# The first range's padding at the end of its scan, and the gate's last 32 channels standing twice in its weights

## The chip, the cores and the metric

The kernel runs on one core of one Trainium2 chip. The metric is the device time of one execution in microseconds; the time of a kernel is the median of its runs. The core's engines are TensorE (PE, with its weight loads shown apart as PEld), VectorE (DVE), ScalarE (ACT), GpSimd (POOL) and SyncE (SP), which issues most DMAs.

## The reference

Two layers of a decoder trunk on 512 tokens, with 16 learned meta tokens ahead of them (T = 528), width 1024. Each layer is half a SwiGLU, a mixer, half a SwiGLU, each on a normalised input and added to the residual. The mixer of layer 0, which the change touches, is RWKV-7 time mixing; the mixer of layer 1 is sparse attention.

```
def rwkv7_time_mix(h, mix, w_r, w_k, w_v, w_o, w0, w1, w2, a0, a1, a2, g1, g2, k_k, k_a, r_k, lnx_g, lnx_b):
    xx = jnp.pad(h, ((0, 0), (1, 0), (0, 0)))[:, :-1] - h          # token before, less this one
    xm = h[None] + xx[None] * mix[:, None, None, :]                # six mixed inputs
    xr, xw, xk, xv, xa, xg = ...
    r, k, v = xr @ w_r, xk @ w_k, xv @ w_v
    w_log = -softplus(-(w0 + tanh(xw @ w1) @ w2)) - 0.5
    a = sigmoid(a0 + (xa @ a1) @ a2)
    g = sigmoid(xg @ g1) @ g2                                      # g1: 1024 x 160, g2: 160 x 1024
    ...                                                            # kk normalised by head, k, decay
    y = wkv7_scan(r, decay, k, v, -kk, kk * a)                     # 16 heads, a 64 x 64 state each
    ...                                                            # group norm of y, bonus r*k*r_k*v
    return ((yn + bonus) * g) @ w_o

def step(S, inp):                                                  # of wkv7_scan, one token
    sa = einsum("bhij,bhj->bhi", S, a_t)
    S = S * w_t + sa * b_t + v_t * k_t
    y = einsum("bhij,bhj->bhi", S, r_t)
```

## The kernel before

**Products.** Every large product is done in three: both operands are split into a rounded high half and a low half (`split`: ACT rounds, DVE subtracts), and `mm3` issues high x high, high x low and low x high into the same accumulator. Weights come as units of 128 x 1024 from one packed array, in the order in which they are used (`Weights`); SP loads `wraw`, ACT rounds it to `whi`, DVE subtracts to `wlo`. `W.take` hands out the blocks and issues the rounding and splitting two units ahead, so the places of the weight splits in ACT's and DVE's program order follow from the takes. PE accumulators are banks named `acc` (4 of them, main work), `bg` (3, side work and gates) and `ry`.

**Ranges and stages.** The tokens are worked in two ranges, A (tokens 0 to 271) and B (272 to 527). The order is: feed-forward 0,0 of A; projections of A (`proj`, stage pA); feed-forward 0,0 of B (stage f00b); output projection of A (`outproj`, oA); projections of B (pB); feed-forward 0,1 of A (f01a); output projection of B (oB); then layer 1.

**Padding.** The scan works in chunks of `CH` = 32 tokens. A has 272 tokens, eight and a half chunks; it gets 16 empty columns (`pad`) ahead of its first token, so that n = 288 and the chunk numbered 0 is half empty. B has n = 256, eight chunks.

**Side chains.** Beside a main stage run generators (`beside`): `prep` (decay powers, keys), `lmat` (for each chunk the masked products of keys and receptances, into `R.G`), `inverse`, `scan`, `bonus` and `post` (group norm). The order of all instructions is fixed while the program is built: `run` asks a planner with prices for each engine (`Clock`) when a chain's next step would be ready, and puts it between two products of the main stage. `drain` issues what is left of the chains at the end of f00b and of f01a, ahead of oA and oB. Every engine then works through its own instructions in that order.

**Inverse.** For each chunk and head a unit triangular 32 x 32 matrix must be inverted. `lmat` writes the matrices to memory with one partition for each pair of chunk and head; `inverse` loads them (16 partitions a chunk), runs through t = `t0` .. 30 with two DVE instructions each, stores the result and loads it back into `R.G`. It does so by parts, `R.parts`, tuples of first chunk, last chunk, and in the kernel before the first row `t0`: for A chunk 0 alone with t0 = 16 (15 steps on 16 partitions), then chunks 1 to 8 (31 steps on 128 partitions); for B chunks 0 to 7 in one part. The scan of a chunk waits for its part; at c = 0 and at each fourth chunk it also waits for the last part before it takes its output tile `ynat`, since the inverse uses tiles of that name. `post` uses a tile `prod`, as the inverse does.

**Scan.** For each chunk: products of the state `S` and of the masked matrices into `ry`, a copy `rs`, a product with the inverse, the new values `uv`, the output into `ynat`, the new state, which is multiplied by the chunk's whole decay `R.PC`. After chunks 3, 7 and the last one, `bonus` and `post` of up to four chunks are put beside.

**Gate.** 160 channels are padded to 256. At the end of `proj` the first matrix is taken as tiles of 128 and of 32 weight columns (lines 938 to 949), and the sigmoid of both goes to `R.sg`. In `outproj` (lines 1270 to 1313) `R.sg` is split to `lhi`, `llo`, and for each of the 8 column tiles `gate(m)` issues three products with 128 rows and three with 32 rows, then a DVE multiply (`tb`), an ACT rounding (`o_hi`) and a DVE subtraction (`o_lo`). Three gates go first; then, for each d, a gate three ahead and the nine products of output tiles 0 to 2 with operand d; after that output tiles 3 to 7.

Of the kernel before, what the change touches and what calls it, by code (L numbers as in the profile page):

```python
# [10 lines left out]
F32 = mybir.dt.float32  # L11
# [6 lines left out]
D = 1024  # L18
DT = 8
# [414 lines left out]
def trunk(ctx, tc, wall, units, h0, vec, cstd, gqk, out, stop=None, gap=0.0, share=400.0, slack=200.0, fulls={}):  # L434
# [67 lines left out]
    def split(hi, lo, src, gp=False):  # L502
        nc.scalar.activation(hi, src, AF.Copy)
        if gp:
            nc.gpsimd.tensor_tensor(lo, src, hi.bitcast(F32), op=OP.subtract)
        else:
            nc.vector.tensor_sub(lo, src, hi.bitcast(F32))
# [278 lines left out]
    class Range:  # L786
        def __init__(self, r):
            self.r = r
            self.pad = 16 if r == A else 0
            self.n = r[1] - r[0] + self.pad  # L790
            self.nch = self.n // CH
            self.have = set()

            self.parts = [(0, 1, 16), (1, 9, 0)] if self.pad else [(0, 8, 0)]
            self.L, self.T = {}, {}

# [5 lines left out]
    def proj(R, norm, sp, core, XB):  # L802

        r, n, pad, nch = R.r, R.n, R.pad, R.nch
        hn2 = [core.tile([128, 4, 1 + 288], F32, name="ynat", bufs=2) for _ in range(2)]
# [10 lines left out]
        xx = [core.tile([128, 4, 288], F32, name="bu", bufs=2) for _ in range(2)]  # L816
        xm, late = {}, []

        def mix(i, d):

            x = work.tile([128, 288], F32, name="tb", bufs=4)
            nc.vector.scalar_tensor_tensor(x[:, :n], xx[d // 4][:, d % 4, :n], col(MIX + 8 * i + d),
                                           hn[d][:, 1:1 + n], op0=OP.mult, op1=OP.add)
            hi = sp.tile([128, 288], F32R, name="xm_hi", bufs=XB)
            lo = sp.tile([128, 288], F32R, name="xm_lo", bufs=XB)

            def make():
                split(hi[:, :n], lo[:, :n], x[:, :n], gp=True)
# [9 lines left out]
        def mixes(k):  # L838
            while k and queue and free[0]:
                i, d = queue.pop(0)  # L840
                if i == 2:
                    norm.apply(d, r, hn[d][:, 1 + pad:1 + n])
                    nc.vector.tensor_sub(xx[d // 4][:, d % 4, :n], hn[d][:, 0:n], hn[d][:, 1:1 + n])
                mix(i, d)
                if i == 2 and pad:
                    nc.vector.tensor_copy(hnlast[:, d], hn[d][:, n:n + 1])
                free[0] -= 1
                k -= 1
# [56 lines left out]
        for kind, *st in proj_steps():  # L905
# [16 lines left out]
            elif kind == "lora":  # L922
                key, d = st
                if pl is None:
                    pl = bbank("ry")
                mm3(pl[:, :n], W.take(blk(key, d, 0)), need(mixof[key], d), st == ["lw", 0], st == ["la", DT - 1])
                free[0] += 1
                mixes(1)
                if st == ["la", DT - 1]:
                    lora_end(pl)  # L930
                yield
            elif kind == "wa2":
                decay(st[0])
# [20 lines left out]
    def prep(R, core):  # L954
# [7 lines left out]
        def pieces(m, p):  # L962
# [18 lines left out]
            nc.scalar.activation(R.PC[:, :nch, m, 0], R.P[:, m, :nch, 32], AF.Copy, scale=math.exp(UP))  # L981
# [74 lines left out]
    def inverse(R, core):  # L1056

        def load(i):
            L = core.tile([128, CH, CH], F32, name="ynat", bufs=2)
            nc.gpsimd.dma_start(L[:16 * (R.parts[i][1] - R.parts[i][0])], R.L[i].rearrange("p c q s t -> (p c q) s t"))  # L1060
            return L
# [6 lines left out]
        for i, (c0, c1, t0) in enumerate(R.parts):  # L1068
# [4 lines left out]
            TT = core.tile([128, CH, CH], F32, name="ynat", bufs=2)  # L1073
            pr = core.tile([128, 1024], F32, name="prod")
            nc.gpsimd.memset(TT[:k], 0.0)
            nc.gpsimd.memset(TT[:k].rearrange("p s t -> p (s t)")[:, 0:1024:33], 1.0)
            yield 5000
            work = 0
            for t in range(t0, CH - 1):
                a, b = t + 1 - t0, CH - 1 - t  # L1080
                pv = pr[:k, :a * b].rearrange("p (a b) -> p a b", b=b)
                dst = TT[:k, t0:t + 1, t + 1:CH]
                nc.vector.tensor_tensor(pv, TT[:k, t0:t + 1, t:t + 1].to_broadcast([k, a, b]),
                                        L[:k, t:t + 1, t + 1:CH].to_broadcast([k, a, b]), op=OP.mult)
                nc.vector.tensor_add(dst, dst, pv)
                work += 150 + 2.1 * a * b
                if work > 500:
                    yield -500
                    work = 0
            nxt = load(i + 1) if ("L", i + 1) in R.have else None  # L1090
            nc.gpsimd.dma_start(R.T[i].rearrange("p c q s t -> (p c q) s t"), TT[:k])
            for n0, n1 in ((c0, c0 + 1), (c0 + 1, c1)):
                for par in range(2):
                    if n0 < n1:
                        nc.gpsimd.dma_start(R.G[64 * par:64 * par + 32, n0:n1, :, 0:32]
                                          .rearrange("s c q t -> s (c q) t"),
                                          R.T[i][par, n0 - c0:n1 - c0].rearrange("c q s t -> s (c q) t"))
            beside(there(i))

    def scan(R, core, S):  # L1100
# [21 lines left out]
        for c in range(R.nch):  # L1122
# [22 lines left out]
            if c % 4 == 3 or not more:  # L1145
                beside(bonus(R, c - c % 4, c % 4 + 1))
# [123 lines left out]
    def outproj(R, sp, nxt):  # L1270

        n, pad, r = R.n, R.pad, R.r
        shi = sp.tile([128, 2, 288], F32R, name="lhi")
        slo = sp.tile([128, 2, 288], F32R, name="llo")
        for i, k in ((0, 128), (1, 32)):
            split(shi[:k, i, :n], slo[:k, i, :n], R.sg[:k, i, :n])
        xs = {}

        def gate(m):
            p = bbank()  # L1280
            for k, q in ((0, 128), (1, 32)):
                w = W.take(blk("g2", k, m))
                mm3(p[:, :n], (w[0][:q], w[1][:q]), (shi[:q, k, :n], slo[:q, k, :n]), k == 0, k == 1)
# [8 lines left out]
        def end(m, p):  # L1292
            residual(m, r, p[:, pad:n], 1.0)
            nxt.add(m, r)
# [437 lines left out]
def lay_out(i):  # L1732
# [24 lines left out]
    mats["g1"] = pad(f["rk_g1"][0], D, 256)  # L1757
    mats["g2"] = pad(f["rk_g2"][0], 256, D)
# [27 lines left out]
```

## Time and profile before

| | us |
|---|---|
| median of 3 runs | 2370.86 (2370.77 to 2374.3) |
| the profiled execution | 2373.61, its span 2371.8 |
| PE busy in it | 2298.7 |
| DVE busy | 1702.1 |
| ACT busy | 1238.7 |
| POOL busy | 169.6 |
| mean granted clock of PE | 0.979 |

How to read it: a row of a timeline has the start, the length, the engine, the line, the operation, and the output and inputs by their names with shapes; in square brackets stands how long the engine was idle before it and what ended that. Products are written weights x rows, then the moving operand: 32*128 32x288 has 32 rows, 128 weight columns and 288 moving columns. Lengths of products overlap, so the pace is read from starts. PEclk is the granted clock as a share of the full one. All instructions carry line 341, that of the recording helper, so they are told apart by their names. In the profile `bg<-lhi,whi` and its like are the gates' products, `acc<-o_hi,whi` the output projection's, `bg<-pa,bd` and `bg<-pb,bd` the bonus's, `bg<-ident,ynat` the transposes of the normalised output.

### The profile page before, as it was taken

How to read it: one execution, taken by the hardware profiler on the slowest of the kernel's cores; microseconds unless marked ns; L12 is line 12 of the kernel's file. 1: busy time of each engine (PE TensorE's matmuls, PEld its weight loads, DVE VectorE, ACT ScalarE, POOL GpSimd, SP SyncE). 2: the span in 40 equal slices, each digit the busy share in tenths (PEclk: the TensorE clock that was granted, in tenths of full speed). 3: DMA queues.
4: the chain of work that ended last, by engine and by line, in shares of the span. 5: the costliest groups of instructions: out<-in, count | busy, mean ns of one | idle time of the engine just before them, and what ended most of it. 6: DMA issues, size and time to landing. Idle time of an engine off the chain costs nothing.

```text
span 2371.8 us, 49461 instructions
## 1 busy us (share of the span) xinstructions
PE 2298.7 (97%) x20122; PEld 2172.6 (92%) x20122; DVE 1702.1 (72%) x3337; ACT 1238.7 (52%) x2109; POOL 169.6 (7%) x215
## 2 busy tenths in 40 slices
PE   8998899999889999999999999999999999999999
PEld 8998889998888899998999999899889788879999
DVE  7667888766787976577565665688767889756665
ACT  5443664456447634654444444455665546644443
POOL 0001521001033111000000000000000000000000
PEclk9999999999899999998999999999999999999999
DMA  6553334542234454243555555454434443326554
GB/s 231 177 175 119 121 130 159 172 148 75 96 120 142 158 161 161 73 134 121 184 172 177 178 187 187 136 185 160 143 125 147 149 154 129 125 81 204 184 182 142
DMA packets 101491, 356.13 MB, mean 150 GB/s; under 512 B 11520, under 2 KB 15632, under 8 KB 101264
## 3 DMA queue, kind: packets, MB, share of 16 engines
q1 hardware_dynamic: 99120, 347.91, 44.5%
q0 software_dynamic: 2144, 5.07, 0.8%
q8 instruction: 158, 2.59, 0.4%
q14 instruction: 69, 0.57, 0.1%
HBM read 348.60 MB, written 4.33 MB: 149 GB/s over the span
## 4 chain that ended last, share of the span: by engine, by line
PE 48%; DVE 5%; ACT 2%; issue 1%; ACTq 0%; DVEq 0%
PE acc L341 43%; PE bg L341 4%; DVE wlo L341 2%; PE ry L341 1%; ACT whi L341 1%; DVE pr L341 0%; DVE m L341 0%; ACT L341 0%; DVE rel L341 0%; DVE tb L341 0%; ACT pr L341 0%; DVE qst L341 0%; DVE h L341 0%; DVE xa_lo L341 0%; ACT pt L341 0%
## 5 line engine op out<-in xcount | busy, mean ns | idle before, releaser
L341 ACT ACTIVATE whi<-wraw 128x1024 fp32r<-128x1024 f32 (+1 forms) x658 | 688.6, 1051 | 472.1 <-PE acc L341 286.7
L341 DVE TENSOR_TENSOR wlo<-wraw,whi 128x1024 fp32r<-128x1024 f32 (+1 forms) x658 | 809.8, 1234 | 165.3 <-ACT whi L341 164.4
L341 PE MATMUL acc<-hid_hi,whi 128*128 128x256 f32 (+1 forms) x1408 | 412.1, 293 | 5.9 <-DVE h L341 5.9
L341 PE MATMUL acc<-hid_lo,whi 128*128 128x256 f32 (+1 forms) x1408 | 401.0, 285 | 0.0
L341 PE MATMUL acc<-hid_hi,wlo 128*128 128x256 f32 (+1 forms) x1408 | 400.7, 285 | 0.0
L341 PE MATMUL acc<-xa_hi,whi 128*128 128x256 f32 (+1 forms) x1088 | 314.5, 289 | 1.6 <-ACT xa_hi L341 1.6
L341 PE MATMUL acc<-x_hi,whi 128*128 128x272 f32 (+1 forms) x1024 | 303.1, 296 | 9.1 <-ACT whi L341 6.6
L341 PE MATMUL acc<-xa_lo,whi 128*128 128x256 f32 (+1 forms) x1088 | 308.8, 284 | 0.8 <-DVE xa_lo L341 0.8
L341 PE MATMUL acc<-xa_hi,wlo 128*128 128x256 f32 (+1 forms) x1088 | 309.0, 284 | 0.1
L341 PE MATMUL acc<-x_hi,wlo 128*128 128x272 f32 (+1 forms) x1024 | 294.6, 288 | 0.2 <-DVE wlo L341 0.2
L341 PE MATMUL acc<-x_lo,whi 128*128 128x272 f32 (+1 forms) x1024 | 294.0, 287 | 0.1
L341 PEld LDWEIGHTS acc<-hid_hi,whi 128*128 128x128 f32 x1408 | 267.2, 190 | 17.9 <-issue 10.9
L341 PEld LDWEIGHTS acc<-hid_lo,whi 128*128 128x128 f32 x1408 | 268.3, 191 | 0.2 <-DVE hid_lo L341 0.2
L341 PEld LDWEIGHTS acc<-hid_hi,wlo 128*128 128x128 f32 x1408 | 267.4, 190 | 0.0
L341 PEld LDWEIGHTS acc<-xa_hi,whi 128*128 128x128 f32 x1088 | 206.4, 190 | 12.8 <-issue 10.3
L341 PE MATMUL acc<-xb_hi,whi 128*128 128x256 f32 x752 | 214.4, 285 | 0.0
L341 PE MATMUL acc<-xb_lo,whi 128*128 128x256 f32 x752 | 210.5, 280 | 0.0
L341 PE MATMUL acc<-xb_hi,wlo 128*128 128x256 f32 x752 | 210.5, 280 | 0.0
L341 PEld LDWEIGHTS acc<-x_hi,whi 128*128 128x128 f32 x1024 | 194.7, 190 | 15.6 <-ACT whi L341 6.6
L341 PEld LDWEIGHTS acc<-xa_lo,whi 128*128 128x128 f32 x1088 | 206.5, 190 | 1.2 <-DVE xa_lo L341 1.2
L341 PEld LDWEIGHTS acc<-xa_hi,wlo 128*128 128x128 f32 x1088 | 206.1, 189 | 0.3 <-DVE wlo L341 0.3
L341 PEld LDWEIGHTS acc<-x_hi,wlo 128*128 128x128 f32 x1024 | 194.5, 190 | 0.7 <-DVE wlo L341 0.7
(295 smaller groups left out, 4357.9 us busy)
## 6 DMA issues: line engine op xcount, KB each, us to landing
wraw<-wall SPq DMA_DIRECT2D x644, 512.0 KB, 3.3
wraw<-wall SPq DMA_DIRECT2D x10, 438.0 KB, 3.2
out<-h SPq DMA_DIRECT2D x8, 256.0 KB, 2.3
h<-h SPq DMA_DIRECT2D x2, 512.0 KB, 8.1
ynat<-L POOLq DMA_DIRECT2D x2, 512.0 KB, 4.8
T<-ynat POOLq DMA_DIRECT2D x2, 512.0 KB, 4.4
L<-gm POOLq DMA_DIRECT2D x14, 64.0 KB, 3.0
gm<-T POOLq DMA_DIRECT2D x4, 224.0 KB, 5.3
```

The costliest lines, as they stand in the source:

```text
L341: r = f(*args, **kw)
```

## The change

The 16 empty columns of A move behind its last token, so the half empty chunk is the last, number 8. The state's decay over that chunk is taken at its 16th column. The inverse is done for chunks 0 to 7 first, then for chunk 8 as 16 x 16 matrices, in tiles of other names (`pz` and the second half of `prod`); the third item of a part is now the size of the matrices. The wait for the last part ahead of `ynat` goes; instead the scan waits, ahead of putting a bonus beside, until all of the inverse is issued.

In the gate's weights the last 32 of the 160 channels stand twice: as columns 128 to 159 and 160 to 191 of the first matrix, and as rows in the same places of the second. The second group's operand then holds the high halves in rows 0 to 31, the low halves in rows 32 to 63 and zeros below, so one product with the high weights gives high x high and high x low, and one with the low weights takes the high halves alone, with zeros in the other rows. All of them are issued with 128 rows.

The diff, cut to its core:

```diff
-            self.parts = [(0, 1, 16), (1, 9, 0)] if self.pad else [(0, 8, 0)]
+            self.parts = [(0, 8, 32), (8, 9, 16)] if self.pad else [(0, 8, 32)]
...
             if pad:
-                nc.gpsimd.memset(hn2[i][:, :, 0:1 + pad], 0.0)
+                nc.gpsimd.memset(hn2[i][:, :, 0:1], 0.0)
+                nc.gpsimd.memset(hn2[i][:, :, 1 + n0:1 + n], 0.0)
...
+        if pad:
+            for i in range(2):
+                nc.gpsimd.memset(xx[i][:, :, n0:n], 0.0)
...
-                for m, k in ((0, 128), (1, 32)):
-                    w = W.take(blk("g1", d, m))
-                    mm3(pg[m][:k, :n], (w[0][:, :k], w[1][:, :k]), x, d == 0, d == DT - 1)
+                for m in range(2):
+                    mm3(pg[m][:, :n], W.take(blk("g1", d, m)), x, d == 0, d == DT - 1)
...
-                    for i, k in ((0, 128), (1, 32)):
+                    for i, k in ((0, 128), (1, 64)):
                         sg = R.sg[:k, i, :n]
...
-            nc.scalar.activation(R.PC[:, :nch, m, 0], R.P[:, m, :nch, 32], AF.Copy, scale=math.exp(UP))
+            nc.scalar.activation(R.PC[:, :8, m, 0], R.P[:, m, :8, 32], AF.Copy, scale=math.exp(UP))
+            if R.pad:
+                nc.scalar.activation(R.PC[:, 8:9, m, 0], R.P[:, m, 8:9, 32 - R.pad], AF.Copy, scale=math.exp(UP))
...
+            if nt == CH:
+                L = core.tile([128, CH, CH], F32, name="ynat", bufs=2)
+            else:
+                L = work.tile([128, 288], F32, name="pz", bufs=1)[:, :nt * nt].rearrange("p (s t) -> p s t", t=nt)
+            nc.gpsimd.dma_start(L[:k], R.L[i].rearrange("p c q s t -> (p c q) s t")[:, :nt, :nt])
...
-            for t in range(t0, CH - 1):
-                a, b = t + 1 - t0, CH - 1 - t
+            for t in range(nt - 1):
+                a, b = t + 1, nt - 1 - t
...
+        R.have.add("inverse")
...
             if c % 4 == 3 or not more:
+                while "inverse" not in R.have:
+                    yield None
                 beside(bonus(R, c - c % 4, c % 4 + 1))
...
             if q == 0:
-                while ("T", len(R.parts) - 1) not in R.have:
-                    yield None
                 ynat = core.tile([128, 16, 64], F32, name="ynat", bufs=2)
...
-        for i, k in ((0, 128), (1, 32)):
-            split(shi[:k, i, :n], slo[:k, i, :n], R.sg[:k, i, :n])
+        nc.gpsimd.memset(shi[64:128, 1].bitcast(F32), 0.0)
+        nc.gpsimd.memset(slo[:, 1].bitcast(F32), 0.0)
+        split(shi[:, 0, :n], slo[:, 0, :n], R.sg[:, 0, :n])
+        nc.scalar.activation(shi[:64, 1, :n], R.sg[:64, 1, :n], AF.Copy)
+        nc.scalar.activation(slo[:32, 1, :n], R.sg[:32, 1, :n], AF.Copy)
+        e = shi[32:64, 1, :n]
+        nc.vector.tensor_sub(e, R.sg[32:64, 1, :n], e.bitcast(F32))
...
-            for k, q in ((0, 128), (1, 32)):
-                w = W.take(blk("g2", k, m))
-                mm3(p[:, :n], (w[0][:q], w[1][:q]), (shi[:q, k, :n], slo[:q, k, :n]), k == 0, k == 1)
+            mm3(p[:, :n], W.take(blk("g2", 0, m)), (shi[:, 0, :n], slo[:, 0, :n]), True, False)
+            w = W.take(blk("g2", 1, m))
+            nc.tensor.matmul(p[:, :n], w[0], shi[:, 1, :n], start=False, stop=False)
+            nc.tensor.matmul(p[:, :n], w[1], slo[:, 1, :n], start=False, stop=True)
...
-            residual(m, r, p[:, pad:n], 1.0)
+            residual(m, r, p[:, :n - pad], 1.0)
...
-    mats["g1"] = pad(f["rk_g1"][0], D, 256)
-    mats["g2"] = pad(f["rk_g2"][0], 256, D)
+    a, b = f["rk_g1"][0], f["rk_g2"][0]
+    mats["g1"] = pad(np.concatenate([a, a[:, 128:]], 1), D, 256)
+    mats["g2"] = pad(np.concatenate([b, b[128:]], 0), 256, D)
```

More of the change, by code (lines that the diff above doesn't have):

```diff
@@ L500, in mm3, with split @@
         nc.tensor.matmul(p, w[1], x[0], start=False, stop=last)
-    def split(hi, lo, src, gp=False):
+    def split(hi, lo, src):
         nc.scalar.activation(hi, src, AF.Copy)
[L504 to L507, printed above, removed]
+        nc.vector.tensor_sub(lo, src, hi.bitcast(F32))
     def newton(y, x, it, a):
@@ L804, in proj @@
         r, n, pad, nch = R.r, R.n, R.pad, R.nch
+        n0 = n - pad
         hn2 = [core.tile([128, 4, 1 + 288], F32, name="ynat", bufs=2) for _ in range(2)]
@@ L827, in make @@
             def make():
-                split(hi[:, :n], lo[:, :n], x[:, :n], gp=True)
+                nc.scalar.activation(hi[:, :n], x[:, :n], AF.Copy)
+                nc.gpsimd.tensor_tensor(lo[:, :n], x[:, :n], hi[:, :n].bitcast(F32), op=OP.subtract)
                 xm[i, d] = (hi[:, :n], lo[:, :n])
@@ L841, in mixes @@
                 if i == 2:
-                    norm.apply(d, r, hn[d][:, 1 + pad:1 + n])
-                    nc.vector.tensor_sub(xx[d // 4][:, d % 4, :n], hn[d][:, 0:n], hn[d][:, 1:1 + n])
+                    norm.apply(d, r, hn[d][:, 1:1 + n0])
+                    nc.vector.tensor_sub(xx[d // 4][:, d % 4, :n0], hn[d][:, 0:n0], hn[d][:, 1:1 + n0])
                 mix(i, d)
                 if i == 2 and pad:
-                    nc.vector.tensor_copy(hnlast[:, d], hn[d][:, n:n + 1])
+                    nc.vector.tensor_copy(hnlast[:, d], hn[d][:, n0:n0 + 1])
                 free[0] -= 1
@@ L1058, in load @@
         def load(i):
-            L = core.tile([128, CH, CH], F32, name="ynat", bufs=2)
-            nc.gpsimd.dma_start(L[:16 * (R.parts[i][1] - R.parts[i][0])], R.L[i].rearrange("p c q s t -> (p c q) s t"))
+            c0, c1, nt = R.parts[i]
+            k = 16 * (c1 - c0)
+            if nt == CH:
[3 more added lines that the diff above has]
+            nc.gpsimd.dma_start(L[:k], R.L[i].rearrange("p c q s t -> (p c q) s t")[:, :nt, :nt])
             return L
@@ L1067, in inverse @@
         nxt = None
-        for i, (c0, c1, t0) in enumerate(R.parts):
+        for i, (c0, c1, nt) in enumerate(R.parts):
             while ("L", i) not in R.have:
@@ L1072, in inverse @@
             k = 16 * (c1 - c0)
-            TT = core.tile([128, CH, CH], F32, name="ynat", bufs=2)
             pr = core.tile([128, 1024], F32, name="prod")
+            if nt == CH:
+                TT = core.tile([128, CH, CH], F32, name="ynat", bufs=2)
+            else:
+                TT = pr[:, 512:512 + nt * nt].rearrange("p (s t) -> p s t", t=nt)
             nc.gpsimd.memset(TT[:k], 0.0)
-            nc.gpsimd.memset(TT[:k].rearrange("p s t -> p (s t)")[:, 0:1024:33], 1.0)
+            nc.gpsimd.memset(TT[:k].rearrange("p s t -> p (s t)")[:, 0:nt * nt:nt + 1], 1.0)
             yield 5000
-            work = 0
-            for t in range(t0, CH - 1):
-                a, b = t + 1 - t0, CH - 1 - t
+            ns = 0
+            for t in range(nt - 1):
+                a, b = t + 1, nt - 1 - t
                 pv = pr[:k, :a * b].rearrange("p (a b) -> p a b", b=b)
-                dst = TT[:k, t0:t + 1, t + 1:CH]
-                nc.vector.tensor_tensor(pv, TT[:k, t0:t + 1, t:t + 1].to_broadcast([k, a, b]),
-                                        L[:k, t:t + 1, t + 1:CH].to_broadcast([k, a, b]), op=OP.mult)
+                dst = TT[:k, 0:t + 1, t + 1:nt]
+                nc.vector.tensor_tensor(pv, TT[:k, 0:t + 1, t:t + 1].to_broadcast([k, a, b]),
+                                        L[:k, t:t + 1, t + 1:nt].to_broadcast([k, a, b]), op=OP.mult)
                 nc.vector.tensor_add(dst, dst, pv)
-                work += 150 + 2.1 * a * b
-                if work > 500:
+                ns += 150 + 2.1 * a * b
+                if ns > 500:
                     yield -500
-                    work = 0
+                    ns = 0
             nxt = load(i + 1) if ("L", i + 1) in R.have else None
-            nc.gpsimd.dma_start(R.T[i].rearrange("p c q s t -> (p c q) s t"), TT[:k])
+            nc.gpsimd.dma_start(R.T[i].rearrange("p c q s t -> (p c q) s t")[:, :nt, :nt], TT[:k])
             for n0, n1 in ((c0, c0 + 1), (c0 + 1, c1)):
@@ L1094, in inverse @@
                     if n0 < n1:
-                        nc.gpsimd.dma_start(R.G[64 * par:64 * par + 32, n0:n1, :, 0:32]
+                        nc.gpsimd.dma_start(R.G[64 * par:64 * par + nt, n0:n1, :, 0:nt]
                                           .rearrange("s c q t -> s (c q) t"),
-                                          R.T[i][par, n0 - c0:n1 - c0].rearrange("c q s t -> s (c q) t"))
+                                          R.T[i][par, n0 - c0:n1 - c0, :, :nt, :nt].rearrange("c q s t -> s (c q) t"))
             beside(there(i))
+        R.have.add("inverse")
     def scan(R, core, S):
```

## The prediction

> **What bounds the kernel now.** I read the page first, then the table of stretches with the granted clock, then the chain of waits, then the timelines of TensorE (PE) and VectorE (DVE) at the places that the diff touches. The page says that PE is the bound:
>
> ```profile
> PE 2298.7 (97%) x20122; PEld 2172.6 (92%) x20122; DVE 1702.1 (72%) x3337; ACT 1238.7 (52%) x2109; POOL 169.6 (7%) x215
> ```
>
> A busy PE isn't a fast one. The stretches (length, PE busy with its instructions, PEclk, DMA share, GB/s) show where the clock is low around the output projections of the first range (A) and of the second (B); the first two lie in the feed-forward stage ahead of A's, the third in A's own, the last two in B's:
>
> ```profile
> 620.00:625.00 5.00, 5.00 (x25) 0.50 0.34 105
> 625.00:628.00 3.00, 3.00 (x28) 0.97 0.00 0
> 632.00:645.00 13.00, 12.02 (x37) 0.50 0.13 42
> 1068.00:1072.00 4.00, 3.10 (x16) 1.00 0.07 15
> 1072.00:1089.00 17.00, 17.00 (x67) 0.51 0.25 89
> ```
>
> For 13 us in A and 17 us in B PE is busy at half its clock, all but 1 us of the 13. Those are just the stretches in which the gate's products with 32 rows stand between the others: they begin with the first gate, and the clock is back when the last gates are issued. The chain of waits has it as PE alone (start, length, engine, count):
>
> ```profile
> 1069.29 5.22 PE bg L341 x23
> 1074.50 2.22 PE acc L341 x9
> 1076.72 1.57 PE bg L341 x6
> ```
>
> Nine products of 256 columns take 2.22 us, 0.247 each, and the six of one gate 1.57 us, 0.262 each. The timeline of PE has the full-speed step, and the ends that I need:
>
> ```profile
> 617.66 0.60 PE L341 MATMUL bg<-pb,bd 128*128 128x32 f32 x4 [1.36 <-ACT pb L341]
> 618.96 1.06 PE L341 MATMUL bg<-pa,bd 128*128 128x32 f32 x4 [0.70 <-ACT pa L341]
> ...
> 628.21 0.28 PE L341 MATMUL acc<-hid_hi,wlo 128*128 128x256 f32 x1
> 630.38 0.65 PE L341 MATMUL bg<-ident,ynat 32*128 32x32 f32 x8 [1.90 <-DVE ynat L341]
> 632.40 0.61 PE L341 MATMUL bg<-lhi,whi 128*128 128x288 f32 x1 [1.37 <-ACT lhi L341]
> ...
> 652.81 0.40 PE L341 MATMUL acc<-o_hi,whi 128*128 128x288 f32 x1
> ...
> 1067.12 0.29 PE L341 MATMUL acc<-hid_lo,whi 128*128 128x272 f32 x1
> 1067.24 0.28 PE L341 MATMUL acc<-hid_hi,wlo 128*128 128x272 f32 x1
> 1068.83 0.38 PE L341 MATMUL bg<-lhi,whi 128*128 128x256 f32 x1 [1.30 <-ACT lhi L341]
> ...
> 1089.53 0.38 PE L341 MATMUL acc<-o_hi,whi 128*128 128x256 f32 x1
> ```
>
> At the end of the feed-forward stage before A (the first four rows) the last chunk's bonus and its normalisation haven't been covered: PE waits 1.36 and 0.70 us in them, 1.90 us for the normalised rows, and in 620 to 625 it runs at half clock. Before B nothing of that kind stands: the stage's last product is at 1067.24 and the gate begins at 1068.83.
>
> **The gate with full rows (both ranges).** Removed: one of six products for each of 8 column tiles in 2 ranges, 16 in all, and the five others now use 128 rows. What I take to be the cause of the half clock is that products of 32 rows count for little as activity. Then the stretch runs at full clock, at 0.12 us a product (1067.12 to 1067.24, 272 columns) in B and 0.13 in A. PE alone would need 40 gate products and 72 of the first three output tiles: 112 x 0.13 = 14.6 us in A, 112 x 0.12 = 13.4 in B. But DVE is late next. Each gate is a multiply on DVE, a rounding on ScalarE (ACT), and a subtraction on DVE that waits for it, one after the other:
>
> ```profile
> 647.18 1.22 DVE L341 TENSOR_TENSOR wlo<-wraw,whi 128x1024 fp32r<-128x1024 f32 x1
> 648.32 0.51 DVE L341 SCALAR_TENSOR_TENSOR tb<-AR,vecs,bg 128x288 f32<-128x288 f32 x1
> 649.34 0.46 DVE L341 TENSOR_TENSOR o_lo<-tb,o_hi 128x288 fp32r<-128x288 f32 x1 [0.51 <-ACT o_hi L341]
> ...
> 1070.62 0.46 DVE L341 SCALAR_TENSOR_TENSOR tb<-AR,vecs,bg 128x256 f32<-128x256 f32 x1
> 1071.57 0.43 DVE L341 TENSOR_TENSOR o_lo<-tb,o_hi 128x256 fp32r<-128x256 f32 x1 [0.48 <-ACT o_hi L341]
> 1071.91 0.47 DVE L341 SCALAR_TENSOR_TENSOR tb<-AR,vecs,bg 128x256 f32<-128x256 f32 x1
> ```
>
> That loop is 1.29 us a gate in B (1070.62 to 1071.91) and about 1.4 in A (648.32 to 649.34, and 0.4 until the next could start). Three weight splits of 1.14 us (647.18 to 648.32) stand among the eight loops. From the first gate product to the first multiply 1.8 us pass (1068.83 to 1070.62, a weight split before it). So the last of the eight operands is there 1.8 + 8 x 1.4 + 3 x 1.14 = 16.4 us after the start in A and 1.8 + 8 x 1.29 + 3 x 1.14 = 15.5 in B, and its nine products end 1.2 and 1.1 us later: 17.6 and 16.6 us. Before, the fifth group of nine starts at 652.81 and at 1089.53, 36 products from the end: 652.81 + 36 x 0.13 - 632.40 = 25.1 us, and 1089.53 + 36 x 0.12 - 1068.83 = 25.0. The gain is 7.5 in A and 8.4 in B, 15.9 together. Bounds: if DVE doesn't bind, 25.1 - 14.6 and 25.0 - 13.4 less 0.5 of start each, 21; if the clock stays low as long as now, what is left is the removed product and the gaps between groups of different rows. In B a period of 9 + 6 products is 3.79 us (2.22 + 1.57), of which 15 x 0.24 (twice 0.12) = 3.6 are products, so a gate loses a product of 0.24 and gaps of 0.2: 0.44 x 16 = 7. So 7 to 21, and I take 15.9, since the loop is the nearest row.
>
> The Trainium skill, TensorE: Matmul & The Clock Gate, would speak against this. Its section Why this matters for your kernels says that a single product of 32 rows takes the same time as one of 128, and Part 1, The HAM clock gate, that sustained busy time releases the clock; the trace disagrees with the second, with 17.00 us busy of 17.00 at 0.51. By the page's rule only the 16 products fewer would count, some 2 us.
>
> **Its preparation.** Two memsets on GpSimd (POOL) for each range, one more ACT copy, and one subtraction that stays. The memsets wait for the buffer's last readers, the stage's last products at 1067.24, and lie beside the square of the last tile and the first rounding on ACT, until 1068.8; only the gate's fourth and fifth product need them. A longer memset than these is in the rows below at 0.98 us, shorter ones at 0.15, so the pair is 0.3 to 2 us against a cover of about 1.6. Uncovered they cost up to 0.5 a range. Nothing else is queued on POOL there. I take 0.2 a range and put it to the 1.8 above.
>
> **The gate's first matrix.** The last tile has 128 instead of 32 weight columns. Steps of PE in that stretch, before:
>
> ```profile
> 337.80 0.29 PE L341 MATMUL acc<-xm_hi,wlo 128*128 128x288 f32 x1
> 337.93 0.30 PE L341 MATMUL acc<-xm_hi,whi 128*32 128x288 f32 x1
> 338.06 0.29 PE L341 MATMUL acc<-xm_lo,whi 128*32 128x288 f32 x1
> ```
>
> Both forms step by 0.13 us. Nothing, up to 0.01 x 48 = 0.5 us if the wider load shows.
>
> **The half chunk at the end.** Now the first range's chain starts with the large triangular inverse (8 chunks, 128 partitions), and the small one (16 partitions, 15 steps) runs beside the scan; the scan does all nine chunks after the large one. Before, the small one stood ahead of the large one, with one chunk's scan done in between. The second range already has the new form, eight chunks with one inverse, so its rows price it (minimum/median/maximum ns, first and last start):
>
> ```profile
> L341 ACT ACTIVATE ynat<-ry x34: 587/591/596, 497.9 to 1026.2; 32x512 f32<-32x512 f32 x34
> ...
> L341 POOL MEMSET ynat<- x8: 148/176/978, 5.0 to 864.9; 128x68 f32 x2, 128x1024 f32 x2, 128x32 f32 x2, 16x1024 f32 x1
> ...
> L341 POOL DMA_DIRECT2D ynat<-L x3: 511/589/597, 412.3 to 863.2; - x3
> ```
>
> ```profile
> 608.74 1.20 ACT L341 ACTIVATE ynat<-ry 32x512 f32<-32x512 f32 x2
> ```
>
> In B the load of the inverse's input is at 863.2 and the scan's last output at 1026.2, 163 us later. In A the first load is at 412.3; with a ninth chunk, (608.74 - 497.9) / 8 = 13.9 us at most, the end comes at 412.3 + 163 + 14 = 589, against 609 now. About 20 us sooner is enough to bring the last bonus and normalisation, which end at 632 now, to 612, under the stage's products, which now end at 628.3. What goes from PE's path: waits of 1.36 + 0.70; the half clock in 620 to 625, 25 products that lose 0.1 us each, 2.5; and the gap between the stage's last product and the gate, counted from a step after the last start, 632.40 - 628.33 = 4.1 against 1068.83 - 1067.36 = 1.5 in B, 2.6. Together 7.2. What takes its place is the wait for the square and rounding on ACT, as in B. But the bonus is issued in program order, and its waits may come along to the new place. I take 5, between 0 and 7.2.
>
> Small pieces: POOL clears six short column blocks for the padding (0.15 us each by the row above) early, with nothing behind them; the last decay of a chunk is copied by two ACT instructions instead of one in A:
>
> ```profile
> L341 ACT ACTIVATE PC<-gm x16: 200/209/223, 327.4 to 831.3; 128x9 f32<-128x9 f32 x8, 128x8 f32<-128x8 f32 x8
> ```
>
> 8 x 0.21 = 1.7 us of ACT, which hides beside PE; without that cover the chain, which has 16 us to spare, takes it. One pair more of stores and one small load and store stand on POOL's queue, about 0.6 us each to issue (the load's row), under the large inverse.
>
> **Sum.** 15.9 + 5 = 20.9 us, less 0.4 of preparation: 20.5. The profiled execution took 2373.6 us (span 2371.8), 2.7 above the median of the runs, 2370.86; from the execution it makes 2353, from the median 2350.4. I forecast 2350 for the median. Nothing behind B's projection is touched.
>
> **Rivals.** (1) The clock comes back, but the waits at the end of A's stage only move: 15.9 alone, 2355. For it: the bonus waits are PE waiting in order for ACT. Against: B's end has none of size. (2) The clock doesn't follow the rows of a product, and stays at half through both gates as now; then 7 + 5, 2359. By the Trainium skill's rule in the paragraph above, with 2 for the gate in place of 7, it would be 2364. For it: half clock begins after idle time (1.30 and 1.37 us) too. Against: idle time alone ends with it, and in B the low clock lasts 17 us of busy PE. (3) The other side: A's scan waits for the whole large inverse, and its chain ends behind the stage; each us of that is a us of PE's path. For a loss the end must pass 628 by more than the 16 us of the gates: 644 where B's pace gives 612, 32 us later; at 650 the time would be 2377. (4) No change within 0.2% (4.7 us), the least that can be told here: the gates bring 7 and A's chain, ending some 7 us behind the stage, takes it back: 2371.
>
> **Chances.** The forecast 0.66, (1) 0.15, (2) 0.12, (3) 0.03, (4) 0.04. Range: 7 for the gates and half of the 5 at the one end, 2361; 21 and 7.2 at the other, 2342. It takes in (1) and (2), 0.93 in all, less what single terms may stray. Faster by more than 0.2%: 0.93; within: 0.04; slower: 0.03.
>
> **What would show it.** In the changed profile: PEclk near 1.00 through both gates but for the first few us; from the first gate product to the end of the first three output tiles 17 to 18 us in place of 25; DVE's loop with no idle before its multiply; PE waiting there for the low half of an operand. A's last scan output near 590 and its normalisation done before the stage's last product. The prediction is wrong if the clock stays at 0.50 with full rows, or if the large inverse in A ends much later than 51 us after its load.

## The result, and the profile after

The changed kernel took 2352.8 us (median of 4 runs, 2348.3 to 2353.2), the kernel before 2370.8 (2370.0 to 2374.3) on the same chip: ratio 0.9917, 95% interval 0.99 to 0.9934, 18 us. A second set of 4 runs on another chip gave 2352.2 (ratio 0.9907, 0.9888 to 0.9926). The profiled execution took 2353.2 us; its page begins

```profile
span 2351.4 us, 49453 instructions
...
PE 2281.8 (97%) x20106; PEld 2161.9 (92%) x20106; DVE 1702.8 (72%) x3337; ACT 1240.7 (53%) x2119; POOL 173.8 (7%) x225
```

against a span of 2371.8 before: 20.4 us between the two profiled executions. PE has 16 instructions fewer and 17 us less of busy time, so most of what went is slow busy time; idle time is 3.5 us less. The stretches of the two gates (length, PE busy, granted clock, DMA share, GB/s), A's ahead of B's:

```profile
627.00:645.00 18.00, 16.01 (x106) 1.00 0.28 96
1060.00:1074.00 14.00, 12.47 (x95) 1.00 0.43 133
```

The clock is 1.00 in both, where it was 0.50 and 0.51. PE is no longer busy all the time there: 2.0 of 18 us, 0.9 of them ahead of the gate's first product, and 1.5 of 14 are waits. The timeline of PE has the ends of the stages, the starts of the gates, their waits, and the last of the 72 products of the first three output tiles:

```profile
612.66 0.39 PE L341 MATMUL acc<-hid_lo,whi 128*128 128x256 f32 x1 [1.77 <-DVE hid_lo L341]
615.54 1.03 PE L341 MATMUL bg<-ident,ynat 32*128 32x32 f32 x8 [0.27 <-DVE ynat L341]
626.37 0.28 PE L341 MATMUL acc<-hid_hi,wlo 128*128 128x256 f32 x1
627.94 0.40 PE L341 MATMUL bg<-lhi,whi 128*128 128x288 f32 x1 [1.30 <-ACT lhi L341]
644.25 0.40 PE L341 MATMUL acc<-o_hi,whi 128*128 128x288 f32 x1 [0.71 <-ACT o_hi L341]
645.78 0.30 PE L341 MATMUL acc<-o_hi,wlo 128*128 128x288 f32 x1
1055.72 0.28 PE L341 MATMUL acc<-hid_hi,wlo 128*128 128x272 f32 x1
1057.31 0.38 PE L341 MATMUL bg<-lhi,whi 128*128 128x256 f32 x1 [1.30 <-ACT lhi L341]
1069.09 0.38 PE L341 MATMUL acc<-o_hi,whi 128*128 128x256 f32 x1 [0.60 <-ACT o_hi L341]
1072.83 0.38 PE L341 MATMUL acc<-o_hi,whi 128*128 128x256 f32 x1 [0.77 <-ACT o_hi L341]
1074.22 0.28 PE L341 MATMUL acc<-o_hi,wlo 128*128 128x256 f32 x1
```

From these starts and those of the profile before, the span is cut into six pieces. (Before, the 72nd product started at 657.56 and 1093.75.)

| stretch | before, us | after, us | difference |
|---|---|---|---|
| start to the last feed-forward product before A's projection | 628.21 | 626.37 | -1.84 |
| from there to A's first gate product | 4.19 | 1.57 | -2.62 |
| A: first gate product to the 72nd product | 25.16 | 17.84 | -7.32 |
| A's 72nd product to the last product before B's gate, and the gap to it | 411.27 | 411.53 | +0.26 |
| B: first gate product to the 72nd product | 24.92 | 16.91 | -8.01 |
| from there to the end of the span | 1278.05 | 1277.18 | -0.87 |

So 15.3 of the 20.4 us come from the gates and 4.5 from the end of A's stage. What binds a gate now is seen on VectorE (DVE): no row has idle time before its multiply (`tb`), and each low half (`o_lo`) waits half a microsecond for ScalarE (ACT):

```profile
630.03 0.51 DVE L341 SCALAR_TENSOR_TENSOR tb<-AR,vecs,bg 128x288 f32<-128x288 f32 x1
631.43 0.51 DVE L341 SCALAR_TENSOR_TENSOR tb<-AR,vecs,bg 128x288 f32<-128x288 f32 x1
...
1059.33 0.47 DVE L341 SCALAR_TENSOR_TENSOR tb<-AR,vecs,bg 128x256 f32<-128x256 f32 x1
1060.29 0.42 DVE L341 TENSOR_TENSOR o_lo<-tb,o_hi 128x256 fp32r<-128x256 f32 x1 [0.48 <-ACT o_hi L341]
1060.63 0.47 DVE L341 SCALAR_TENSOR_TENSOR tb<-AR,vecs,bg 128x256 f32<-128x256 f32 x1
```

A loop is 1.40 us in A (630.03 to 631.43) and 1.30 in B. The head of the chain of waits from 1055 to 1076 names DVE and ACT, where before it named PE alone from 1069 on. The loop's operations (`tb`, `o_hi`, `o_lo`) have a third of it; the weight splits (`wlo`, `whi`), which stand in the same two queues, have 42%, PE 5.4%.

```profile
by line: DVE wlo L341 27.9%; ACT whi L341 14.5%; ACT o_hi L341 12.0%; DVE tb L341 11.5%; DVE o_lo L341 10.1%; PE acc L341 5.4%; issue 4.7%; DVE h L341 3.8%; ACT last L341 2.0%; ACT tb L341 2.0%; DVE llo L341 2.0%; DVE lhi L341 2.0%; ACT ss 
```

At the end of A's stage the half clock has not gone. Of four stretches of 2.5 us the two between these are at 0.50:

```profile
612.50:615.00 2.50, 2.34 (x14) 0.72 0.63 208
...
620.00:622.50 2.50, 2.50 (x22) 0.91 0.47 146
```

A mean of 0.72 is half clock for 56% of the first stretch, 0.91 for 18% of the last: from 613.6 to 620.45, 6.85 us. Read in the same way in stretches of 1 us, it lay from 618.3 to 625.2 before, 6.8 us: it has moved, and is no shorter.

### The profile page after: what moved, and what is told of

The parts are those of the page before. It is cut to its first block, busy times and chain, and to the rows that moved or that the text cites. A ratio compares the mean times of both kernels' runs of the same rounds, so it can differ in the third digit from the quotient of the medians.

```text
span 2351.4 us, 49453 instructions
## 1 busy us (share of the span) xinstructions
PE 2281.8 (97%) x20106; PEld 2161.9 (92%) x20106; DVE 1702.8 (72%) x3337; ACT 1240.7 (53%) x2119; POOL 173.8 (7%) x225
## 4 chain that ended last, share of the span: by engine, by line
PE 83%; DVE 10%; ACT 4%; issue 2%; DMA 1%; POOL 0%; SPq 0%; ACTq 0%; DVEq 0%; POOLq 0%
PE acc L341 71%; PE bg L341 9%; PE ry L341 4%; DVE wlo L341 3%; DVE tb L341 2%; ACT whi L341 1%; DMA wraw<-wall 1%; DVE h L341 0%; DVE pr L341 0%; DVE ynat L341 0%; DVE m L341 0%; ACT L341 0%; DVE rel L341 0%; DVE bu L341 0%; ACT pr L341 0%
## 5 line engine op out<-in xcount | busy, mean ns | idle before, releaser
L341 ACT ACTIVATE whi<-wraw 128x1024 fp32r<-128x1024 f32 (+1 forms) x658 | 688.5, 1051 | 460.1 <-PE acc L341 286.6
```

The costliest lines, as they stand in the source:

```text
L341: r = f(*args, **kw)
```

## The experiments

The theory: products of 32 rows, as many as stood among the others, kept the clock at half through the gates; with full rows the clock stays up, and DVE's loop takes over as the bound. The rivals: the product that was saved, or the way the operands are prepared, brings the time; or the scan's part brings it. The kernel before ran again beside each group of experiments; a ratio is to those runs.

**Each part alone.** First the gate's part on the kernel before, without the scan's:

```
-            for k, q in ((0, 128), (1, 32)):
-                w = W.take(blk("g2", k, m))
-                mm3(p[:, :n], (w[0][:q], w[1][:q]), (shi[:q, k, :n], slo[:q, k, :n]), k == 0, k == 1)
+            mm3(p[:, :n], W.take(blk("g2", 0, m)), (shi[:, 0, :n], slo[:, 0, :n]), True, False)
+            w = W.take(blk("g2", 1, m))
+            nc.tensor.matmul(p[:, :n], w[0], shi[:, 1, :n], start=False, stop=False)
+            nc.tensor.matmul(p[:, :n], w[1], slo[:, 1, :n], start=False, stop=True)
...
+    mats["g1"] = pad(np.concatenate([a, a[:, 128:]], 1), D, 256)
+    mats["g2"] = pad(np.concatenate([b, b[128:]], 0), 256, D)
```

> The gate's part of the change alone; the padding stays ahead of A's tokens. Theory (products of 32 rows hardly count as activity, so the clock halves; with 128 rows it stays full and DVE's loop of multiply, rounding and subtraction is late next): from the first gate product to the end of the first three output tiles 18 us in A and 17 in B in place of 25, PEclk near 1.00 in B, and a time of 2356 (15 less than before). The waits at the end of A's stage stay as they were. Rival (the clock follows idle time, or the number of products, not their rows): half clock stays in both gates, and the time is 2364 to 2369.

Measured 2361.2 us (2359.6 to 2361.9, 4 runs), ratio 0.9941 (0.9923 to 0.9959), 11.8 us less. The forecast of 15 less was missed: in the profiles the two gates give 14.7 us, but the rest of the span is 3.0 longer, which isn't placed. The two stretches from the first gate product to the 72nd were 18.5 and 16.9 us. The first was not at full clock from the start, for the half clock stood there from 631 on, ahead of the gate; the second was (A's gate began at 633.28, B's at 1063.69):

```profile
631.00:637.50 6.50, 4.67 (x21) 0.50 0.19 73
638.00:652.00 14.00, 13.41 (x99) 1.00 0.38 131
1064.00:1081.00 17.00, 15.37 (x115) 1.00 0.36 120
```

Then the scan's part alone, the whole change with those lines of the gate as they were before:

> The padding at the end of A's scan alone; the gate as before. Theory: the gate of A starts about 4.5 us sooner than before and then runs at half clock as before, the time is 2366. Rival (the two parts help each other, so that neither alone brings its share): within 1 us of before, 2371. If the whole gain came from here it would be 2353.

Measured 2360.0 us (2355.0 to 2363.4, 4 runs), ratio 0.993 (0.9907 to 0.9953), 12.9 less where 4.5 was expected. A's gate began 6.5 us sooner than before (625.88), more than in the whole change, and the unchanged gates, too, were shorter, 22.3 and 23.4 us for 25.2 and 24.9. The rows say why: the half clock in them lasted about 7 and 14 us.

```profile
629.50:636.00 6.50, 6.50 (x24) 0.50 0.18 69
1062.50:1076.50 14.00, 14.00 (x56) 0.51 0.31 107
```

So the half clock in a gate with 32-row products has no fixed length, and the parts don't add: 11.8 + 12.9 = 24.7 against 18 to 21 for both. Its lengths come in steps, though. Summed over stretches of half a microsecond, the time at half clock in each of the twelve profiles, around the end of A's stage (602 to 627), A's gate (626 to 660) and B's (1050 to 1095), is 0 or, within 0.07 us, 1, 2, 4, 5 or 6 times 3.41 us.

**Rows, number of products, or preparation.** The kernel before, all six products kept, the operands of the second three filled with zeros to 128 rows (the weights' block has zeros there already):

```
+        nc.gpsimd.memset(shi[:, 1].bitcast(F32), 0.0)
+        nc.gpsimd.memset(slo[:, 1].bitcast(F32), 0.0)
...
-            for k, q in ((0, 128), (1, 32)):
+            for k, q in ((0, 128), (1, 128)):
```

> The kernel before, with the 32-row operands of the gate filled with zeros to 128 rows: six products for each gate as before, all of 128 rows, and nothing else changed. Theory: full clock in B's gate, the length of both gates set by DVE's loop as in the changed kernel, 17 to 19 us, time 2356 to 2358. Rival (what helps is the product fewer): no better than before, 25 us and 2371. Rival (a product counts by the values that it multiplies, so zero rows count for nothing): half clock as before, 2369 to 2371.

Measured 2360.9 us (2359.2 to 2362.1, 4 runs), ratio 0.994 (0.9923 to 0.9958): the gain of the gate's part without saving a product and without new arithmetic, from rows of zeros. Stretches 19.6 and 16.7 us; B's clock:

```profile
1063.00:1080.00 17.00, 15.87 (x121) 1.00 0.36 117
```

The product that the change saves is therefore worth nothing measurable in B (16.7 with six, 16.9 with five): DVE's loop binds in both, again with no idle time before a multiply.

The counterpart: the whole change, its two products for the last 32 channels cut to 32 rows. Without the low halves of those channels' operands there are still five products, as in the change.

```
-            nc.tensor.matmul(p[:, :n], w[0], shi[:, 1, :n], start=False, stop=False)
-            nc.tensor.matmul(p[:, :n], w[1], slo[:, 1, :n], start=False, stop=True)
+            nc.tensor.matmul(p[:, :n], w[0][:32], shi[:32, 1, :n], start=False, stop=False)
+            nc.tensor.matmul(p[:, :n], w[1][:32], slo[:32, 1, :n], start=False, stop=True)
```

> The changed kernel with the second pair of each gate cut to 32 rows; this leaves the product of high weights and low operand of the last 32 channels out. Five products for each gate, two of them of 32 rows. Theory: half clock is back for most of the gate, 21 to 24 us in place of 17 to 18, PEclk 0.5 to 0.7 in B, time 2360 to 2366. Rival (the number of products): as the changed kernel, 2353.

Measured 2366.3 us, ratio 0.996 (0.9942 to 0.9977); 10 runs lay from 2353.4 to 2370.4, a spread of 17 us that no kernel with full rows showed. The profiled execution (2370.4, the longest) has the half clock through both gates, 20 us in B, with PE busy all the while; its gates took 25.7 and 25.5 us, where 21 to 24 were expected. Yet one of the ten executions took 2353.4 us at a mean granted clock of 0.984, the values of the kernel with full rows (0.978 in the profiled one): with two such products the half clock is frequent, not certain.

```profile
629.00:645.00 16.00, 16.00 (x58) 0.50 0.25 89
1066.00:1086.00 20.00, 20.00 (x81) 0.50 0.32 103
```

**Where the effect begins.** The same two products cut to 64 rows, which keeps the result complete:

```
+            nc.tensor.matmul(p[:, :n], w[0][:64], shi[:64, 1, :n], start=False, stop=False)
+            nc.tensor.matmul(p[:, :n], w[1][:64], slo[:64, 1, :n], start=False, stop=True)
```

> The whole change, with the second pair of every gate cut from 128 to 64 rows; the result stays complete, and the number of products too. Theory (the clock follows the rows that are at work, in proportion): of five products three have 128 rows and two 64, a mean of 102 against 77 at best with 32-row products before; the clock is at half speed for part of the stretches, 2355 to 2360. Rival (a threshold between 32 and 64 rows, or only products of 32 rows are hurtful): full clock in both, 2353.

Measured 2350.8 us (2349.1 to 2352.6, 4 runs), ratio 0.9904 (0.9888 to 0.9921). The expected half clock didn't come; the stretches were 18.3 and 16.9 us. (The mean of 77 in the expectation would count 32 rows as none; the six products of the kernel before have a mean of 80.)

```profile
625.00:642.00 17.00, 17.00 (x105) 1.00 0.36 115
1055.00:1071.00 16.00, 15.92 (x110) 1.00 0.38 120
```

PE also steps more slowly where it changes between full and fewer rows: 0.20 us in place of 0.12 in this kernel (1059.78 to 1059.98), which kept the full clock. So these gaps alone don't bring the half clock.

And only the last of the five products cut to 32 rows:

> The whole change, with only the last of the five products of every gate cut to 32 rows; the result stays complete. Of 14 products in a period one has 32 rows. Theory (activity adds up over a stretch, and a few products of 32 rows among full ones do no harm): full clock through both gates, 2351 to 2354, as unaltered (2352.2 on the chip before) or with 64 rows in two products (2350.8). Rival (every 32-row product sets the clock back for a step of some 3.4 us, however few there are): half clock for 10 us or more in each gate, as with two such products, 2358 to 2368.

Measured 2351.5 us (2350.8 to 2358.3, 4 runs), ratio 0.9913 (0.9888 to 0.9938), with clock 1.00 in 623 to 641 and in 1053 to 1069. So in the profiled execution one 32-row product among 14 does no harm. It was the fastest of the four, though, at a mean clock of 0.987; the slowest took 2358.3 us at 0.982, and no profile shows where its clock was low.

By the rows at work in a period of nine products and a gate, as a share of full rows, 0.946 with one of 32 rows (13 x 128 + 32 of 14 x 128) and 0.929 with two of 64 ran at full clock; 0.893 with two of 32, and 0.85 before (12 x 128 + 3 x 32 of 15 x 128), ran at half for 6.8 to 20.5 us of a gate. But the share of a period doesn't settle it. In the profile before, A's half clock stood ahead of the gate's first product (632.40), and was over at 645.7. A's last three gates, with 32-row products among the same others, ran at 1.00:

```profile
632.00:633.00 1.00, 0.60 (x1) 0.50 0.02 8
650.00:651.00 1.00, 1.00 (x7) 1.00 0.95 389
...
647.48 0.39 PE L341 MATMUL bg<-lhi,whi 32*128 32x288 f32 x1
652.59 0.29 PE L341 MATMUL bg<-lhi,wlo 32*128 32x288 f32 x1
```

In B it began at 1072.3, 3.5 us after the first gate product. At the start of either range four gates stand in a row before the first group of nine, with shares of 0.625 before, 0.70 with two of 32 rows, 0.80 with two of 64 and 0.85 with one of 32. So a limit on the share in a period, one on the share in these first gates, and one on the number of 32-row products are all open, and so is what brought the clock back in A.

**DVE's loop.** If the loop binds, taking ACT's rounding out of it must shorten the gates:

```
-            split(hi[:, :n], lo[:, :n], t[:, :n])
+            while lows:
+                lows.pop()()
+            nc.scalar.activation(hi[:, :n], t[:, :n], AF.Copy)
+            lows.append(lambda: nc.vector.tensor_sub(lo[:, :n], t[:, :n], hi[:, :n].bitcast(F32)))
...
+            elif lows:
+                lows.pop()()
```

> The whole change, and the subtraction that makes the low half of an operand is issued one gate later, behind the next gate's multiply, so that VectorE's loop no longer holds the wait for ScalarE's rounding. Changed kernel: 2352.8. Theory (with the clock at full speed the loop VectorE - ScalarE - VectorE binds the gates, 1.3 to 1.4 us each, and TensorE waits there for rounded halves, 0.6 to 0.8 us at a time): the loop falls to about 1 us, the two stretches from 17.8 and 16.9 us to about 15 and 14, near 112 products at 0.13 and 0.12, so 2348, 4 to 6 us less. Rival (the stretches are bound by TensorE or by weights arriving and the loop is only an accompaniment): 2352 to 2353, no change.

Measured 2347.6 us (2345.1 to 2349.6, 4 runs), ratio 0.989 (0.9873 to 0.9907). The unaltered change, run beside it,

> The whole change once more, unaltered, for its spread on this chip beside the other three: 2348 to 2354 if the phase of the clock's steps moves it as little as in its first runs; a spread of 10 us or more, as with 32-row products, if the full-row gate too depends on that phase.

took 2352.2 (2350.0 to 2353.7): 4.6 us between the medians, and the two sets don't overlap. The stretches fell to 15.6 and 14.0 us, 5.1 less together, with PE busy for 14.93 of 15 and 13.92 of 14 us in them; the chain of waits from 1051 to 1068 is led by PE again, and while the first gates run its pieces (start, length) are nothing else:

```profile
by line: PE bg L341 27.5%; PE acc L341 23.3%; DVE wlo L341 14.4%; ACT whi L341 12.4%; DVE h L341 4.7%; issue 3.5%; DVE llo L341 2.6%; ACT last L341 2.5%; DVE ss L341 2.5%; ACT tb L341 2.5%; DVE tb L341 2.3%; ACT ss L341 2.0%; ACT lhi L341 1
...
1057.23 0.58 PE bg L341 x5
1057.81 1.06 PE acc L341 x9
1058.87 0.59 PE bg L341 x5
```

A period is 1.64 us there, 14 products at 0.117. This is the faster version that the profile pointed to.

**The end of A's stage.** The wait of 1.77 us for a low half stands behind some ten small DVE operations of the last chunk's normalisation. Two edits move them. One lets the planner give the side chains less lead in that stage (2500 ns; 3000 where the table has no entry):

```
-FULL = {"pA": 2000.0, "pB": 1500.0, "f01a": 1500.0, "kvqA": 1500.0, "f10b": 1500.0, "f11a": 3000.0}
+FULL = {"pA": 2000.0, "pB": 1500.0, "f00b": 2500.0, "f01a": 1500.0, "kvqA": 1500.0, "f10b": 1500.0, "f11a": 3000.0}
```

> The whole change, with a smaller lead of VectorE and ScalarE allowed to the side chains in the feed-forward stage ahead of the first projection (2500 in place of 3000 ns by the planner's count). It touches only where the scan's steps stand among that stage's products. Theory (the 1.77 us wait for a low half at 612.66 and the half clock of 613.6 to 620.3 that begins with it are paid because a run of some ten small VectorE operations of the last normalisation stands in front of the feed-forward's own): that wait becomes shorter than 1 us and the half clock there goes, 2 to 4 us less than the changed kernel, 2349 to 2351. Rival (the waits only move: less lead puts the chain's end later, and the wait comes in another place of the stage's end): 2352 to 2356, with another wait of 1 to 2 us in the stage's last 20 us.

Measured 2355.7 us (2353.7 to 2358.0, 4 runs), 3.5 more than the unaltered change beside it. The wait went and three others came, 0.91 us for a rounding at 613.04 and the two below, with half clock both there (6.83 us) and in A's gate (3.41):

```profile
618.53 0.60 PE L341 MATMUL bg<-ident,ynat 32*128 32x32 f32 x4 [1.55 <-DVE ynat L341]
620.86 0.60 PE L341 MATMUL bg<-ident,ynat 32*128 32x32 f32 x4 [1.72 <-DVE AR L341]
```

The other, on top of the later subtraction, moves that run of ten operations behind the low half:

```
+        if k == 1:
+            yield 3000
         newton(rs, va, it[:n], tt)
```

> The whole change with the subtraction one gate later (2347.6 before this edit), and the last chunk's normalisation, half a chunk's rows, is told to issue its run of ten small VectorE operations 3 us of TensorE's time after its sum of squares. On VectorE the feed-forward's weight split and the low half that TensorE waited 1.78 us for then stand in front of that run. Theory (that run, 2.3 us, in front of the low half is what TensorE waits for at 611.9, and the half clock of 612.4 to 615.9 that follows comes from this wait): the wait shrinks under 0.5 us and the half clock goes, 1.5 to 3 us less, 2344.5 to 2346. Rival (the delay moves on: the normalised rows and the transposes behind them come later, and TensorE waits there or at the stage's end): 2347 to 2350, with a wait of over 1 us at a transpose.

Measured 2346.4 us (2344.4 to 2349.4, 6 runs), ratio 0.9884 (0.9863 to 0.9905): not to be told from 2347.6 without it. The 1.78 us wait and the half clock behind it went, as the theory had it. But PE then waited for the residual sums, which the ten operations now delayed, and the gap between the stage's last product and the gate grew by 1.3 us. The clock was 1.00 in 617 to 624, and 0.50 in the gate, 627 to 630; another 3.41 us at half clock came at 1088, behind B's gate, where the kernel without this edit had none:

```profile
616.91 0.38 PE L341 MATMUL acc<-hid_hi,whi 128*128 128x256 f32 x1 [1.50 <-DVE h L341]
626.55 0.40 PE L341 MATMUL bg<-lhi,whi 128*128 128x288 f32 x1 [2.61 <-ACT lhi L341]
...
617.00:624.00 7.00, 6.94 (x56) 1.00 0.33 102
627.00:630.00 3.00, 2.96 (x12) 0.50 0.13 20
```

The rival's "moves on" is right, its place (a transpose) wrong. That the half clock comes from the wait alone, as both theories have it, doesn't hold either. The kernel with one 32-row product has the same wait of 1.77 us at this place, with PE busy for only 0.73 of the 2.5 us around it, and stayed at full clock throughout:

```profile
609.35 0.39 PE L341 MATMUL acc<-hid_lo,whi 128*128 128x256 f32 x1 [1.77 <-DVE hid_lo L341]
...
607.50:610.00 2.50, 0.73 (x6) 1.00 0.07 8
```

Seven profiles have a wait of 1.77 to 1.88 us at this place. Behind it one has no half clock (this one), four have 3.41 us of it, and the change has 6.83 in both its profiles.

## Why the prediction was right, and where it wasn't

Forecast 20.5 us from the profiled execution, 2353; its successor took 2353.2. The 2350 for the median took off the 2.7 us by which that execution lay above its median; the execution after lay 0.4 above its own. Of the 2.8 us between forecast and median these make 2.3, and rounding most of the rest; it is no step of the working.

- **Gate with full rows: right, shown.** 17.6 and 16.6 us forecast, 17.84 and 16.91 measured. The cause (rows) holds in three runs: zeros in full rows keep the clock, fewer products with 32 rows lose it, 64 rows keep it. The prediction read more from the profile before than it shows: the half clock does not begin with the first gate and end with the last ones. In A it was there before the first gate product and gone with three gates to come; in B it came 3.5 us into the gates. The bound (DVE's loop) holds in the run with the later subtraction, which came to 15.6 and 14.0 where the working's bound for PE alone was 14.6 and 13.4 plus the start. One sign came out otherwise: PE waits in the gates for the rounded high half (`o_hi`), not for the low half.
- **Rival (2), the clock doesn't follow the rows: fell.** What spoke for it, that half clock begins after idle time, holds in A. With full rows, too, it is there, from 631.0 in the gate's part alone and from 632.8 with zeros, for 6.83 us each against 13.65 before. In B's gate no profile without two or three 32-row products has any. The milder form by the Trainium skill (TensorE: Matmul & The Clock Gate, Part 1, The HAM clock gate), by which sustained busy time is enough to release the clock, fell too: PE was busy for 20.00 of 20.00 us at 0.50 with two 32-row products. The same section says that activity is judged over a free-running window of about 3.4 us; the 6.85 us of half clock at the end of A's stage is two of those, and agrees, as do the steps of 3.41 us in the other profiles.
- **Preparation: the 0.2 us a range right, their place wrong.** The memsets took 0.34 us each and were done by 627.5, before the gate began at 627.94; they cost nothing. But from the first gate product to the first multiply it is 2.02 us in B for 1.79 before, since the two subtractions on DVE take 0.90 us up to the weight split and took 0.67; why they now stand further apart, no run shows (POOL after; DVE in B after, then before):

```profile
626.76 0.34 POOL L341 MEMSET lhi<- 64x288 f32 x1 [30.64 <-PE acc L341]
...
1057.29 0.42 DVE L341 TENSOR_TENSOR llo<-sg,lhi 128x256 fp32r<-128x256 f32 x1 [0.45 <-ACT lhi L341]
...
1058.19 1.23 DVE L341 TENSOR_TENSOR wlo<-wraw,whi 128x1024 fp32r<-128x1024 f32 x1
...
1068.81 0.75 DVE L341 TENSOR_TENSOR llo<-sg,lhi 128x256 fp32r<-128x256 f32 x2 [0.46 <-ACT lhi L341]
1069.48 1.21 DVE L341 TENSOR_TENSOR wlo<-wraw,whi 128x1024 fp32r<-128x1024 f32 x1
```

- **The scan's end: right.** 589 forecast, 590.14 measured; the large inverse was stored 53.0 us after its input's load (412.78 to 465.78), near the 51 allowed. The normalisation, too, ended ahead of the stage's last product (618.1 for 626.37), so rivals (3) and (4), by which A's chain ends behind the stage, fell.

```profile
590.14 1.19 ACT L341 ACTIVATE ynat<-ry 32x512 f32<-32x512 f32 x2 [1.85 <-PE ry L341]
...
412.78 0.58 POOL L341 DMA_DIRECT2D ynat<-L  x1
...
465.78 0.56 POOL L341 DMA_DIRECT2D T<-ynat  x1 [49.29 <-DVE h L341]
```

- **The end of A's stage: the sum right, its make-up wrong.** The failed step is "what goes from PE's path: waits of 1.36 + 0.70; the half clock in 620 to 625". In their place stand 1.77 + 0.27, and a half clock of 6.85 us, as long as before: for these pieces rival (1) came true. The normalisation's last rows were written at 618.1 (616.79 + 1.34, its last multiplies), not 612. What did go is the gap before the gate, 2.62 for 2.6. The other 1.84 lies earlier, where the prediction had nothing. PE idles less under the scan (the first row is before, the second after):

```profile
550.00:600.00 50.00, 48.67 (x807) 1.00 0.22 73
...
550.00:600.00 50.00, 50.00 (x729) 1.00 0.31 97
```

In this stretch two of the scan's products waited 0.82 and 0.38 us for `bu` before and none does after; the scan stands elsewhere among the stage's products now. If PE's 1.33 us less of idle time is kept to the end of the stage, it is 1.3 of the 1.84; the rest isn't placed. So that 4.5 came out near the forecast 5, and with it the sum of 20.5 near 20.4, is in part luck. Nor is 4.5 a firm size: in the seven kernels profiled with this scan and the unaltered lead, A's gate began between 622.50 and 627.94 (the latest in the profile used above), in the three with the old scan between 632.36 and 633.28. Single profiles thus give 4.4 to 10.8 us. The seven follow the half clock at the end of the stage: 622.50 with none, 624.44 to 625.88 with 3.41 us, 627.01 and 627.94 with 6.83. Six of them have the same code up to A's gate, so among these the difference comes with the execution and not with the edits.

## What to carry to other kernels

Look at the granted clock beside PE's busy share: full busy time at half clock that lies over one kind of product points to that kind, here products with few rows, and filling them up, even with zeros, can be worth more than saving some. Then cost the loop of the next engine before taking the full gain: here PE alone would have let 10.5 and 11.6 us go, and 7.3 and 8.0 went until the wait for ACT was taken out of DVE's order. A wait that comes from DVE's order at the end of a stage was moved by both edits of that order, with nothing gained: count the whole queue of the stage against its length first.

## What wasn't expected of the hardware

- Rows of zeros count as work for the clock: full clock in 1063 to 1080 with three of a gate's six products three quarters zeros.
- The half clock came in steps of 3.41 us, and in gates with 32-row products in no fixed number of them: 13.65 and 17.07 us before, 6.83 and 13.65 in the scan's part alone, whose gates are the same, 17.07 and 20.48 with two such products. The runs spread accordingly: over 17 us with two such products, over 14 in one set of the kernel before (2368.6 to 2382.6, 11 runs), over 7.5 with one, over 2 to 5 in every kernel with rows full or of 64.
- The length of a wait didn't settle whether half clock followed. Waits of 0.6 to 0.8 us inside full-row gates left the clock at 1.00, and so did the 1.30 ahead of each of B's gates with full rows; one of 1.77 at the end of A's stage was followed by 6.83 us of half clock in two profiles and by none in a third. Where PE's waits fall against the steps of 3.41 us may decide it; no run tests that.
